# A hybrid decoder layer on one core: the sums from the output projection on move from GpSimd to VectorE, and the last norm's column sums are written earlier

## The chip, the core and the metric

The kernel runs on one core of a Trainium2 chip. The metric is the device time of one execution in microseconds. The engines named below are TensorE (PE in the rows, its weight loads PEld), VectorE (DVE), ScalarE (ACT), GpSimd (POOL) and SyncE (SP, the queue that issues the transfers). Each has its own queue of instructions and works it off in order; semaphores tie the queues together.

## The reference

One layer of a decoder in fp32, 1024 tokens by 1024 channels. The parts that come last, and that the change is about:

```python
h = h + mix @ w_out                                              # output projection
u = rms_norm(h, norm_mlp_g)
h = h + jnp.square(jax.nn.relu(u @ w_up)) @ w_down               # up and down, 4096 wide
gate = jax.nn.sigmoid(rms_norm(h, norm_ple_g) @ w_ple_gate)
h = h + gate * (p @ w_ple)                                       # gate
return rms_norm(h, final_norm_g)                                 # last norm
```

`mix` is the output of eight attention heads and four mLSTM heads; the change does not touch them.

## The kernel before

**Arithmetic.** Activations lie transposed, channels on partitions and tokens along the row, so a tile is 128 channels by 1024 tokens (two halves of 512). Each fp32 operand is kept as a high part and a low part: `split` casts the high part on ScalarE (L92) and takes source minus high part on VectorE (L93). `mm3` (L101 to L103) makes three matmuls of it: high by high, high by low, low by high.

**Seven products.** Up, down and gate are computed in 2x2 blocks with seven products instead of eight. Their keys are b11, t1, t2, b22, t3, b21, t4; the t operands are sums of blocks, on the side of the weights and on the side of the activations. These sums, in SBUF, are what moves:
- `load_blocks` (L754) loads the weights of one output block of up (`wu`, 32 calls) or of the gate (`wpg`) and forms the weight sums, L759 to L761: one of 128x512 and two of 128x256. Those of `wu` run on GpSimd, those of `wpg` on VectorE already. Then it splits a part of 768 columns, which the first products of the next block use, and one of 1024.
- `operands` (L788) forms the sums of h for up, L797: sixteen of 128x512, four after the 4th and four after the 8th output channel block (each on two halves), in the midst of the output projection.
- `weights` (L962) forms, while the down projection runs, the weight sums of 128x1024: L968 for t1 (8), L975 for t2 and b22 (16, each one needs the tile `s` of the key before), L971 for t3 (8). Weights arrive by `wd_r` (four buffers, 512 KB each) and activations by `y_r` (three). A sum frees a buffer of `wd_r`, and SP's next transfer into it waits for that.
- `gate` (L1132) adds the squares for the last norm: L1146, five of them on GpSimd.

**Down.** For each key there are eight steps g; a step takes one tile of weights and one of activations, splits both (`wd`, `y`), and runs 24 matmuls of 128x512. At a key's last step the sums in PSUM are added into h on VectorE (L1085).

**The end.** The last 256 columns of both halves are done last. `final_cols(i)` (L1169) takes column sums on TensorE (`cs`) of one quarter of the tokens, forms their mean on VectorE (`ra`, L1180) and the power on GpSimd (`rb`, L1181). `final(i)` (L1183) spreads `rb` over the partitions by TensorE (`bp`), copies it (`rows`) and multiplies: eight tiles `out`, on VectorE (L1195) for the numbers in `ON_V`, otherwise on ScalarE (L1197) and GpSimd (L1198); then SP writes them out (L1201), 1 MB a quarter.

**Order.** The source is not the order of execution. A scheduler places the instructions of each engine by a simulation of its own at build time; the tile pools add the waits for free buffers. On the chip the order of an engine is fixed.

Of the kernel before, what the change touches and what calls it, by code (L numbers as in the profile page):

```python
# [12 lines left out]
ALU = mybir.AluOpType  # L13
# [3 lines left out]
P = 128  # L17
D = 1024
T = 1024
KT = D // P  # L20
# [25 lines left out]
def layer_kernel(ctx, tc, xT, wqk, wv, wvg, wmv, wmqk, wmo, wout, wup, wdown, wpg, wple, pT,  # L46
                 cols, cosT, sinT, biasT, identT, maskT, lastT, belowT, outT):
    nc = tc.nc
    V, S, G, PE = nc.vector, nc.scalar, nc.gpsimd, nc.tensor
# [3 lines left out]
    op = ctx.enter_context(tc.tile_pool(name="op", bufs=14))  # L53
# [8 lines left out]
    def unit(name, dt=F32R):  # L62
        return op.tile([P, T], dt, name=name, tag="op")
# [24 lines left out]
    def split(hl, src, scale=None):  # L88

        hi, lo = hl  # L90
        if scale is None:
            S.copy(hi, src)  # L92
            V.tensor_tensor(lo, src, hi.bitcast(F32), op=ALU.subtract)  # L93
        else:
            S.activation(hi, src, AF.Copy, scale=scale)
            V.scalar_tensor_tensor(lo, src, scale, hi.bitcast(F32), op0=ALU.mult, op1=ALU.subtract)
        return hl
# [87 lines left out]
    for i in range(2):  # L185
        raw = unit("wr", F32)
        w0.append([wp.tile([P, WT], F32R, name="wqk_" + t, tag="w" + t) for t in "hl"])
        for at in ((slice(0, 256), slice(256, T)) if i == 0 else (slice(0, T),)):
# [7 lines left out]
            if i == 0 and at.start == 0:  # L196
                x0 = pair("x")
                for c in range(NCH):
                    sl = slice(c * CH, (c + 1) * CH)
# [4 lines left out]
    for k in range(KT):  # L204
# [5 lines left out]
        eng = G if k in (1, 3) else V  # L210
# [310 lines left out]
    L = 2 * P  # L521
# [192 lines left out]
    with ExitStack() as tail:  # L714
# [36 lines left out]
        WI = dict(b11=0, t1=1, t2=2, b21=3, t4=4, t3=5, b22=6)  # L751
        BANK = dict(b11="x", t1="z", t2="x", b22="z", t3="x", b21="y", t4="x")

        def load_blocks(src, name, raw=None, pool=None, eng=G):  # L754
            if raw is None:
                raw = wtc.tile([P, 8, L], F32, name=name + "_r", tag="wc", bufs=2)
            if src is not None:
                nc.sync.dma_start(raw[:, :4], src)
            eng.tensor_tensor(raw[:, 4:7:2], raw[:, 2:3].to_broadcast([P, 2, L]), raw[:, 1:4:2], op=ALU.subtract)  # L759
            eng.tensor_tensor(raw[:, 5], raw[:, 3], raw[:, 4], op=ALU.subtract)  # L760
            eng.tensor_tensor(raw[:, 7], raw[:, 0], raw[:, 5], op=ALU.subtract)  # L761
            wa = split(wtile(name, 3, "wa", pool), raw[:, 3:6])
            wb = wtile(name, 4, "wb", pool)
            split([t.rearrange("p (a b) l -> p a (b l)", b=2) for t in wb],
                  raw.rearrange("p (a b) l -> p a (b l)", b=2)[:, 0::3])
            return wa, wb
# [21 lines left out]
        def operands(src, new, temp):  # L788

            ts = {k: temp("t") for k in ("t1", "t3", "t2", "t4")}  # L790
            c0, c1 = slice(0, CH), slice(CH, T)
            for key, i0, s0, i1, s1, o in (("t1", 0, c1, 0, c0, ALU.subtract), ("t2", 1, c1, "t1", None, ALU.add),
                                           ("t3", 0, c1, 1, c1, ALU.add), ("t4", 1, c0, "t2", None, ALU.subtract)):
                for u in range(2):
                    us = slice(u * CH, (u + 1) * CH)
                    in1 = ts[i1][:, us] if s1 is None else src[u][i1][:, s1]
                    G.tensor_tensor(ts[key][:, us], src[u][i0][:, s0], in1, op=o)  # L797
            x = {}
            for key in OPS:
                hl = x[key] = new()  # L800
                if key in ts:
                    split(hl, ts[key])
                    continue
                i, at = dict(b11=(0, c0), b21=(1, c0), b22=(1, c1))[key]
                for u in range(2):
                    us = slice(u * CH, (u + 1) * CH)
                    split((hl[0][:, us], hl[1][:, us]), src[u][i][:, at])
            return x
# [56 lines left out]
        for k2 in range(KT // 2):  # L865
            e = ztile("emb")
            for i in range(2):
                k = 2 * k2 + i
# [91 lines left out]
        sw = [sp4[g // 2][g % 2] for g in range(NG)]  # L960

        def weights(key, g):  # L962

            if key in ("b11", "b21", "t4"):
                return wraw(g, dict(b11=A11, b21=A12, t4=A22)[key])
            if key == "t1":
                a, b = wraw(g, A21), wraw(g, A22)
                G.tensor_tensor(sw[g], a, b, op=ALU.subtract)  # L968
            elif key == "t3":
                a, b = wraw(g, A21), wraw(g, A11)  # L970
                G.tensor_tensor(a, a, b, op=ALU.subtract)  # L971
                return a
            else:
                a = wraw(g, dict(t2=A11, b22=A12)[key])
                G.tensor_tensor(sw[g], a, sw[g], op=ALU.subtract)  # L975
            return sw[g]

        h = [unit("h", F32) for _ in range(KT)]
# [81 lines left out]
        for key in D_OPS:  # L1060
# [4 lines left out]
            i, c = TO_C[key]  # L1065
            for g in range(NG):
# [5 lines left out]
                if (key, g) in LOADS:  # L1072

                    k, half_of = LOADS[key, g]
                    G.tensor_copy(h[k][:1, half_of.start:half_of.start + 1], yl.bitcast(F32)[:1, :1])
                    nc.sync.dma_start(h[k][:, half_of], hs[k, :, half_of])
                for o in range(KT // 2):
                    for u in range(2):
                        at = slice((2 * o + u) * P, (2 * o + u + 1) * P)
                        us = slice(u * CH, (u + 1) * CH)  # L1080
# [14 lines left out]
                if (key, g) == ("t4", 5):  # L1095
                    raws = [act.tile([P, 2, T], F32, name="wpg_r", tag="act").rearrange("p a (b l) -> p (a b) l", l=L)
                            for _ in range(2)]
                    for i in range(2):
# [4 lines left out]
        wt0, wt1, wcp, xb = [tail.enter_context(tc.tile_pool(name=n, bufs=b, reuse_waits="tile"))  # L1103
                             for n, b in (("wt0", 1), ("wt1", 1), ("wcp", 2), ("xb", 4))]
# [3 lines left out]
        fin = state  # L1108
        wblocks = {}

        def fetch(o):
            wblocks[o] = []
            for i in range(2):
                if o == 0:
                    raw, src = raws[i], None
                else:
                    raw, src = wcp.tile([P, 8, L], F32, name="wpg_r", tag="wc"), wpg[o, i]
                    if o == 1:

                        G.tensor_copy(raw[:1, 0, :1], X[i]["t4"][1].bitcast(F32)[:1, :1])  # L1120
                wblocks[o].append(load_blocks(src, "wpg", raw, (wt0, wt1)[i], V))

        def fetch_emb(o):
            ahead = unit("e", F32) if o == 0 else None
# [7 lines left out]
        def gate(k, sl, src, ga):  # L1132
            c = sl.start // CH
            at = slice(sl.start - c * CH, sl.stop - c * CH)
            V.tensor_tensor(ga, src, rB[:, sl], op=ALU.mult)
            S.activation(ga, ga, AF.Tanh, scale=0.5)
            V.scalar_tensor_tensor(ga, ga, 1.0, emb[k, c][:, at], op0=ALU.add, op1=ALU.mult)
            V.scalar_tensor_tensor(h[k][:, sl], ga, 0.5, h[k][:, sl], op0=ALU.mult, op1=ALU.add)
            if k == 0:
                S.activation(fin[:, sl], h[k][:, sl], AF.Square)  # L1140
                return
            S.activation(ga, h[k][:, sl], AF.Square)
            if k == KT - 1:
                last[sl.start] = ga
            else:
                (G if c and k < 6 else V).tensor_tensor(fin[:, sl], fin[:, sl], ga, op=ALU.add)  # L1146

        def embed(o, off=0, n=CH, hooks={}):
            tmp = {}
# [19 lines left out]
        def final_cols(i):  # L1169
            sl = FINAL[i]  # L1170
            nt = (sl.stop - sl.start) // P
            cs = acc_tile("cs3")
            for j in range(nt):
                for src in (fin[:, sl], last[sl.start]):
                    PE.matmul(cs[:, j:j + 1], src[:, j * P:(j + 1) * P], ones, start=src is not last[sl.start],
                              stop=src is last[sl.start])
            a = zp.tile([P, nt], F32, name="ra3", tag="ra")
            b = cols_of[i] = zp.tile([P, nt], F32, name="rb3", tag="rb")
            at = slice(sl.start // P, sl.stop // P)
            V.scalar_tensor_tensor(a, cs[:, :nt], 1.0 / D, seps[:, at], op0=ALU.mult, op1=ALU.add)  # L1180
            G.tensor_tensor(b, a, mhalf[:, :nt], op=ALU.pow)  # L1181

        def final(i):  # L1183
            sl = FINAL[i]
            n = sl.stop - sl.start
            bp = acc_tile("bp3")
            bcast_rows(bp, cols_of[i], n // P)
            rows = small("rows")[:, :n]
            S.copy(rows, bp[:, :n])
            outs = wcp.tile([P, 8, L], F32, name="out", tag="wc")  # L1190
            for k in range(KT):
                o = outs[:, k]
                gain = col[:, C_GFIN + k:C_GFIN + k + 1]
                if k in ON_V[i]:
                    V.scalar_tensor_tensor(o, h[k][:, sl], gain, bp[:, :n], op0=ALU.mult, op1=ALU.mult)  # L1195
                else:
                    S.mul(o, h[k][:, sl], gain)  # L1197
                    G.tensor_tensor(o, o, rows, op=ALU.mult)  # L1198
                if k + 1 in TO[i]:
                    k0 = max(t for t in (0,) + TO[i] if t <= k)  # L1200
                    nc.sync.dma_start(outT[k0:k + 1, :, sl].rearrange("k p t -> p k t"), outs[:, k0:k + 1])  # L1201

        ON_V = ((0, 1, 3, 4, 6), (0, 1, 3, 4, 5, 6), range(KT), (0, 2, 3, 5, 6, 7))
        TO = ((4, 8), (4, 8), (4, 8), (2, 4, 6, 8))
        FINAL = [slice(c * CH + a, c * CH + a + L) for a in (0, L) for c in (1, 0)]

# [8 lines left out]
        for o in range(1, NO - 1):  # L1215
# [4 lines left out]
        fetch_emb(NO - 1)  # L1220
        embed(NO - 1, 0, L)
        embed(NO - 1, L, L, hooks={"b11": [lambda: final_cols(0)], "b22": [lambda: final(0)],
                                   "t3": [lambda: final_cols(1)], "t4": [lambda: final(1), lambda: final_cols(2)]})
        final(2)
        final_cols(3)
        final(3)


def _tables():
# [78 lines left out]
```

## Time and profile before

| | |
|---|---|
| median of 3 runs | 1397.48 us (1396.22 to 1398.34) |
| profiled execution | 1397.32 us, span 1395.5 us |
| output projection, late half | about 583 to 627 us of the span |
| embedding product `pl` | about 627 to 650 us |
| up | about 650 to 985 us |
| down | about 985 to 1290 us |
| gate | about 1295 to 1376 us |
| last norm and output | to 1395.5 us |

In the page's busy times VectorE counts the time in which an instruction is held, as well as that in which it works; GpSimd's spans are rough. The clock of TensorE that the throttle granted stands in the rows of stretches as 1.00 (2.4 GHz) or 0.50 (1.2 GHz).

### The profile page before, as it was taken

Reading aid. Unit: us, or ns where it says so; the run is one execution under the profiler, and the core shown is the slowest. Engines: PE = TensorE matmul, PEld = TensorE weight load, DVE = VectorE, ACT = ScalarE, POOL = GpSimd, SP = SyncE. Lnnn points to the kernel's source line nnn. Section 1 sums busy time; section 2 is a strip of 40 time slices with the busy share of each in tenths; the row PEclk is TensorE's granted clock in tenths of the full one; section 3 lists DMA queues with packets and bytes.
Section 4 is the critical chain, followed back from the end, with each engine's and each line's share of the span. In section 5 each row is a group of like instructions: output and inputs, shape, how many; then the busy total and the mean of one; then the engine's idle time right before and its main releaser. Section 6 shows DMA issues by size and latency. Waiting matters only on the chain.

```text
span 1395.5 us, 18439 instructions
## 1 busy us (share of the span) xinstructions
PE 1337.2 (96%) x6795; PEld 1121.1 (80%) x6795; DVE 1018.9 (73%) x1558; ACT 654.7 (47%) x1036; POOL 408.2 (29%) x271
## 2 busy tenths in 40 slices
PE   8999999999979999999999999999999899999995
PEld 6978988977868887787888888888887688888875
DVE  7788679589859796597566676567558965778896
ACT  6556545644446343256443334435334233465553
POOL 1432031142103222056333443332006771311012
PEclk9999999999999999999999999999999999999997
DMA  6111012222225347554164444446869674481323
GB/s 231 46 50 37 22 51 62 61 91 84 76 71 196 128 138 241 200 185 179 46 223 154 166 157 175 151 152 253 322 231 322 245 247 144 151 301 61 106 83 128
DMA packets 79017, 208.25 MB, mean 149 GB/s; under 512 B 7536, under 2 KB 19728, under 8 KB 74320
## 3 DMA queue, kind: packets, MB, share of 16 engines
q1 hardware_dynamic: 78928, 207.09, 43.1%
q8 instruction: 53, 0.87, 0.3%
q14 instruction: 36, 0.29, 0.1%
HBM read 146.74 MB, written 60.32 MB: 148 GB/s over the span
## 4 chain that ended last, share of the span: by engine, by line
PE 50%; DVE 11%; DMA 7%; issue 3%; POOL 2%; ACT 2%; SPq 0%; DVEq 0%; POOLq 0%; ACTq 0%
PE u L102 7%; PE u L103 7%; PE u L101 7%; PE d L102 6%; PE d L103 6%; PE d L101 6%; DMA wd_r<-wdown 2%; DMA w<-arow 1%; DMA wpg_r<-wpg 1%; POOL s L968 1%; DVE yl L93 1%; DMA in<-mixmd 1%; PE mo L101 1%; PE o L103 1%; PE mo L103 1%
## 5 line engine op out<-in xcount | busy, mean ns | idle before, releaser
L102 PE MATMUL u<-x,wuh 128*128 128x512 f32 x448 | 178.4, 398 | 0.2 <-DVE x L93 0.2
L101 PE MATMUL u<-x,wuh 128*128 128x512 f32 x448 | 176.0, 398 | 1.5 <-ACT x L92 1.5
L102 PE MATMUL d<-yl,wdh 128*128 128x512 f32 x432 | 169.0, 392 | 7.3 <-DVE yl L93 7.3
L103 PE MATMUL u<-x,wul 128*128 128x512 f32 x448 | 173.4, 398 | 0.0
L103 PE MATMUL d<-yh,wdl 128*128 128x512 f32 x432 | 168.3, 391 | 0.0
L101 PE MATMUL d<-yh,wdh 128*128 128x512 f32 x432 | 166.6, 391 | 0.0
L93 DVE TENSOR_TENSOR wul<-wu_r,wuh 128x768 fp32r<-128x768 f32 (+1 forms) x64 | 72.3, 1130 | 78.8 <-ACT wuh L92 78.8
L101 PEld LDWEIGHTS u<-x,wuh 128*128 128x128 f32 x448 | 84.9, 190 | 22.6 <-ACT x L92 2.4
L102 PEld LDWEIGHTS d<-yl,wdh 128*128 128x128 f32 x432 | 81.5, 189 | 25.9 <-DVE yl L93 8.9
L102 PEld LDWEIGHTS u<-x,wuh 128*128 128x128 f32 x448 | 85.0, 190 | 20.7 <-DVE x L93 0.5
L759 POOL TENSOR_TENSOR wu_r<-wu_r 128x512 f32<-128x512 f32 x32 | 47.0, 1468 | 186.3 <-DMA wu_r<-wup 161.2
L103 PEld LDWEIGHTS u<-x,wul 128*128 128x128 f32 x448 | 85.0, 190 | 20.1
L92 ACT CAST wuh<-wu_r 128x768 fp32r<-128x768 f32 (+1 forms) x64 | 60.5, 946 | 78.7 <-POOL wu_r L760 55.2
L103 PEld LDWEIGHTS d<-yh,wdl 128*128 128x128 f32 x432 | 81.6, 189 | 16.9
L101 PEld LDWEIGHTS d<-yh,wdh 128*128 128x128 f32 x432 | 81.4, 189 | 16.9
L93 DVE TENSOR_TENSOR yl<-y_r,yh 128x1024 fp32r<-128x1024 f32 x54 | 89.8, 1664 | 0.0
L93 DVE TENSOR_TENSOR wdl<-wd_r,wdh 128x1024 fp32r<-128x1024 f32 x30 | 42.5, 1416 | 51.3 <-ACT wdh L92 51.3
L412 ACT ACTIVATE pr<-pr,mn 128x128 f32<-128x128 f32 (+3 forms) x64 | 49.5, 774 | 56.0 <-PE av L415 30.4
L92 ACT CAST wdh<-wd_r 128x1024 fp32r<-128x1024 f32 x30 | 31.5, 1051 | 73.4 <-PE d L102 54.2
L92 ACT CAST wdh<-s 128x1024 fp32r<-128x1024 f32 x24 | 25.2, 1048 | 84.1 <-issue 70.5
L911 ACT COPY tmp<-u 128x512 f32<-128x512 f32 x48 | 28.0, 586 | 77.9 <-PE u L103 77.9
L93 DVE TENSOR_TENSOR wdl<-s,wdh 128x1024 fp32r<-128x1024 f32 x24 | 37.3, 1555 | 36.1 <-ACT wdh L92 36.1
(398 smaller groups left out, 3754.0 us busy)
## 6 DMA issues: line engine op xcount, KB each, us to landing
wd_r<-wdown SPq DMA_DIRECT2D x72, 512.0 KB
y_r<-zd SPq DMA_DIRECT2D x56, 512.0 KB
wu_r<-wup SPq DMA_DIRECT2D x32, 512.0 KB
zd<-zz SPq DMA_DIRECT2D x16, 1024.0 KB
zd<-zt SPq DMA_DIRECT2D x16, 1024.0 KB
wm_r<-wmqk SPq DMA_DIRECT2D x8, 512.0 KB
wo_r<-wout SPq DMA_DIRECT2D x16, 256.0 KB
hs<-h SPq DMA_DIRECT2D x8, 512.0 KB
```

The source lines that it names most:

```text
L92: S.copy(hi, src)
L93: V.tensor_tensor(lo, src, hi.bitcast(F32), op=ALU.subtract)
L101: PE.matmul(ps, wh, xh, start=start, stop=False, skip_group_check=more)
L102: PE.matmul(ps, wh, xl, start=False, stop=False, skip_group_check=more)
L103: PE.matmul(ps, wl, xh, start=False, stop=stop, skip_group_check=more)
L412: S.activation(pr[:, :nk], pr[:, :nk], AF.Exp, scale=-1.0, bias=mn[:, :1], accum_out=den)
L759: eng.tensor_tensor(raw[:, 4:7:2], raw[:, 2:3].to_broadcast([P, 2, L]), raw[:, 1:4:2], op=ALU.subtract)
L911: S.copy(tmp[key], ps)
L968: G.tensor_tensor(sw[g], a, b, op=ALU.subtract)
```

## The change

All sums named above go to VectorE: `load_blocks` loses its argument for the engine, `operands`, `weights` and `gate` call `V`. What stays on GpSimd from there on are the powers (L831, L833, L1181), copies of one element that hold back a load (L1075, L1120), and products of the last norm (L1198). For quarter 2 VectorE takes five tiles `out` instead of eight; for quarter 1 still six, of which one is another. `final(1)` moves from the hook of the last product to the end, and `final_cols(3)` before it.

```diff
@@ -751,14 +751,14 @@
-        def load_blocks(src, name, raw=None, pool=None, eng=G):
+        def load_blocks(src, name, raw=None, pool=None):
             if raw is None:
                 nc.sync.dma_start(raw[:, :4], src)
-            eng.tensor_tensor(raw[:, 4:7:2], raw[:, 2:3].to_broadcast([P, 2, L]), raw[:, 1:4:2], op=ALU.subtract)
-            eng.tensor_tensor(raw[:, 5], raw[:, 3], raw[:, 4], op=ALU.subtract)
-            eng.tensor_tensor(raw[:, 7], raw[:, 0], raw[:, 5], op=ALU.subtract)
+            V.tensor_tensor(raw[:, 4:7:2], raw[:, 2:3].to_broadcast([P, 2, L]), raw[:, 1:4:2], op=ALU.subtract)
+            V.tensor_tensor(raw[:, 5], raw[:, 3], raw[:, 4], op=ALU.subtract)
+            V.tensor_tensor(raw[:, 7], raw[:, 0], raw[:, 5], op=ALU.subtract)
             wa = split(wtile(name, 3, "wa", pool), raw[:, 3:6])
@@ -794,7 +794,7 @@
                     in1 = ts[i1][:, us] if s1 is None else src[u][i1][:, s1]
-                    G.tensor_tensor(ts[key][:, us], src[u][i0][:, s0], in1, op=o)
+                    V.tensor_tensor(ts[key][:, us], src[u][i0][:, s0], in1, op=o)
             x = {}
@@ -965,14 +965,14 @@
                 a, b = wraw(g, A21), wraw(g, A22)
-                G.tensor_tensor(sw[g], a, b, op=ALU.subtract)
+                V.tensor_tensor(sw[g], a, b, op=ALU.subtract)
             elif key == "t3":
                 a, b = wraw(g, A21), wraw(g, A11)
-                G.tensor_tensor(a, a, b, op=ALU.subtract)
+                V.tensor_tensor(a, a, b, op=ALU.subtract)
                 return a
                 a = wraw(g, dict(t2=A11, b22=A12)[key])
-                G.tensor_tensor(sw[g], a, sw[g], op=ALU.subtract)
+                V.tensor_tensor(sw[g], a, sw[g], op=ALU.subtract)
             return sw[g]
@@ -1118,7 +1118,7 @@
                         G.tensor_copy(raw[:1, 0, :1], X[i]["t4"][1].bitcast(F32)[:1, :1])
-                wblocks[o].append(load_blocks(src, "wpg", raw, (wt0, wt1)[i], V))
+                wblocks[o].append(load_blocks(src, "wpg", raw, (wt0, wt1)[i]))
@@ -1143,7 +1143,7 @@
             else:
-                (G if c and k < 6 else V).tensor_tensor(fin[:, sl], fin[:, sl], ga, op=ALU.add)
+                V.tensor_tensor(fin[:, sl], fin[:, sl], ga, op=ALU.add)
@@ -1200,7 +1200,7 @@
-        ON_V = ((0, 1, 3, 4, 6), (0, 1, 3, 4, 5, 6), range(KT), (0, 2, 3, 5, 6, 7))
+        ON_V = ((0, 1, 3, 4, 6), (0, 1, 3, 4, 6, 7), (0, 1, 3, 4, 6), (0, 2, 3, 5, 6, 7))
         TO = ((4, 8), (4, 8), (4, 8), (2, 4, 6, 8))
@@ -1220,10 +1220,10 @@
         embed(NO - 1, L, L, hooks={"b11": [lambda: final_cols(0)], "b22": [lambda: final(0)],
-                                   "t3": [lambda: final_cols(1)], "t4": [lambda: final(1), lambda: final_cols(2)]})
-        final(2)
+                                   "t3": [lambda: final_cols(1)], "t4": [lambda: final_cols(2)]})
         final_cols(3)
-        final(3)
+        for i in range(1, 4):
+            final(i)
```

Three places show how the order of VectorE changes. First the down projection, where key b21 ends and t1 begins. L93 are the low parts (`wdl` of weights, `yl` of activations, in the order of their steps), `s_8967` to `s_8970` the sums of two steps each. VectorE before:

```order
L93 TENSOR_TENSOR wdl_9534<-wd_r_9531,wdh_9533 128x1024
L93 TENSOR_TENSOR yl_9528<-y_r_9525,yh_9527 128x1024
L93 TENSOR_TENSOR wdl_9591<-s_8967,wdh_9590 128x1024
L93 TENSOR_TENSOR yl_9582<-y_r_9579,yh_9581 128x1024
L93 TENSOR_TENSOR wdl_9630<-s_8967,wdh_9629 128x1024
L1085 TENSOR_TENSOR h_8971<-h_8971,d_9261 128x512
L93 TENSOR_TENSOR yl_9621<-y_r_9618,yh_9620 128x1024
L1085 TENSOR_TENSOR h_8973<-h_8973,d_9262 128x512
L1085 TENSOR_TENSOR h_8975<-h_8975,d_9263 128x512
L1085 TENSOR_TENSOR h_8977<-h_8977,d_9264 128x512
```

and now:

```order
L968 TENSOR_TENSOR s_8968<-wd_r_9663,wd_r_9665 128x1024
L93 TENSOR_TENSOR wdl_9591<-s_8967,wdh_9590 128x1024
L968 TENSOR_TENSOR s_8968<-wd_r_9704,wd_r_9706 128x1024
L93 TENSOR_TENSOR yl_9582<-y_r_9579,yh_9581 128x1024
L93 TENSOR_TENSOR wdl_9630<-s_8967,wdh_9629 128x1024
L968 TENSOR_TENSOR s_8969<-wd_r_9745,wd_r_9747 128x1024
L1085 TENSOR_TENSOR h_8971<-h_8971,d_9261 128x512
L93 TENSOR_TENSOR yl_9621<-y_r_9618,yh_9620 128x1024
L1085 TENSOR_TENSOR h_8973<-h_8973,d_9262 128x512
L1085 TENSOR_TENSOR h_8975<-h_8975,d_9263 128x512
L968 TENSOR_TENSOR s_8969<-wd_r_9786,wd_r_9788 128x1024
L1085 TENSOR_TENSOR h_8977<-h_8977,d_9264 128x512
```

The sums L968 for the steps of t1 stand between the low parts and between the additions into h (L1085) of the key before, each about one step ahead of the low part `wdl` that reads it.

Next a cycle of up, where `zz` and `zt` are the results of the block before and `wu_r_7731`, `wu_r_7744` the two weight tiles of the next. VectorE before:

```order
L891 SCALAR_TENSOR_TENSOR zz_7464<-zz_7464,rB_7034 128x2048
L896 TENSOR_TENSOR zt_7591<-zz_7464 128x512
L898 TENSOR_TENSOR zt_7591<-zz_7464 128x512
L919 TENSOR_TENSOR zz_7597<-tmp_7666,u_7639 128x512
L93 TENSOR_TENSOR wul_7737<-wu_r_7731,wuh_7736 128x768
L897 TENSOR_TENSOR zt_7591<-zz_7464,zt_7591 128x512
L93 TENSOR_TENSOR wul_7750<-wu_r_7744,wuh_7749 128x768
```

and now:

```order
L891 SCALAR_TENSOR_TENSOR zz_7464<-zz_7464,rB_7034 128x2048
L759 TENSOR_TENSOR wu_r_7731<-wu_r_7731 128x2x256
L759 TENSOR_TENSOR wu_r_7744<-wu_r_7744 128x2x256
L760 TENSOR_TENSOR wu_r_7731<-wu_r_7731 128x256
L760 TENSOR_TENSOR wu_r_7744<-wu_r_7744 128x256
L761 TENSOR_TENSOR wu_r_7731<-wu_r_7731 128x256
L896 TENSOR_TENSOR zt_7591<-zz_7464 128x512
L898 TENSOR_TENSOR zt_7591<-zz_7464 128x512
L761 TENSOR_TENSOR wu_r_7744<-wu_r_7744 128x256
L919 TENSOR_TENSOR zz_7597<-tmp_7666,u_7639 128x512
L93 TENSOR_TENSOR wul_7737<-wu_r_7731,wuh_7736 128x768
```

The six sums of the next block's weights stand between the stores of the block before; the second L759 stands ahead of work that does not read its tile.

Last the end, after the last product's additions; `h_8978` and `ga_12107` belong to the last tile, `bp3` to a quarter. VectorE before:

```order
L1195 SCALAR_TENSOR_TENSOR out_12118<-h_8971,col_70,bp3_12113 128x256
L1195 SCALAR_TENSOR_TENSOR out_12118<-h_8972,col_70,bp3_12113 128x256
L1195 SCALAR_TENSOR_TENSOR out_12118<-h_8974,col_70,bp3_12113 128x256
L1195 SCALAR_TENSOR_TENSOR out_12118<-h_8975,col_70,bp3_12113 128x256
L1195 SCALAR_TENSOR_TENSOR out_12118<-h_8976,col_70,bp3_12113 128x256
L1195 SCALAR_TENSOR_TENSOR out_12118<-h_8977,col_70,bp3_12113 128x256
L1137 SCALAR_TENSOR_TENSOR ga_12087<-ga_12087,e_11828 128x256
L1138 SCALAR_TENSOR_TENSOR h_8978<-ga_12107,h_8978 128x256
L1180 SCALAR_TENSOR_TENSOR ra3_12136<-cs3_12131,seps_80 128x2
L1138 SCALAR_TENSOR_TENSOR h_8977<-ga_12087,h_8977 128x256
L1146 TENSOR_TENSOR state_8979<-state_8979,ga_12087 128x256
```

and now:

```order
L1138 SCALAR_TENSOR_TENSOR h_8977<-ga_12087,h_8977 128x256
L1137 SCALAR_TENSOR_TENSOR ga_12107<-ga_12107,e_11830 128x256
L1138 SCALAR_TENSOR_TENSOR h_8978<-ga_12107,h_8978 128x256
L1146 TENSOR_TENSOR state_8979<-state_8979,ga_12087 128x256
L1180 SCALAR_TENSOR_TENSOR ra3_12118<-cs3_12113,seps_80 128x2
L1195 SCALAR_TENSOR_TENSOR out_12136<-h_8971,col_70,bp3_12131 128x256
L1195 SCALAR_TENSOR_TENSOR out_12136<-h_8972,col_70,bp3_12131 128x256
L1180 SCALAR_TENSOR_TENSOR ra3_12127<-cs3_12122,seps_80 128x2
L1195 SCALAR_TENSOR_TENSOR out_12136<-h_8974,col_70,bp3_12131 128x256
L1195 SCALAR_TENSOR_TENSOR out_12136<-h_8975,col_70,bp3_12131 128x256
L1195 SCALAR_TENSOR_TENSOR out_12136<-h_8977,col_70,bp3_12131 128x256
```

The six `out` of quarter 1 stood ahead of the last L1137 and L1138; now they stand behind them and behind the last L1146, and the mean (L1180) of a later quarter stands among them.

## Rows read from the trace of the kernel before

**Rows 1.** page, busy time: engine, us (share of the span), instructions
```profile
PE 1337.2 (96%) x6795; PEld 1121.1 (80%) x6795; DVE 1018.9 (73%) x1558; ACT 654.7 (47%) x1036; POOL 408.2 (29%) x271
```

**Rows 2.** waits of TensorE, whole span: us in total, times, longest
```profile
PE d L102 <- DVE yl L93: 7.3, 4, 3.5
...
PE bp L130 <- POOL rb L1181: 6.8, 3, 3.2
...
PE u L101 <- ACT x L92: 1.5, 1, 1.5
...
PE pg L101 <- ACT wpgh L92: 1.2, 1, 1.2
```

**Rows 3.** timeline of VectorE, 1076 to 1102 us: start, us, instruction, [idle before]
```profile
1076.98 1.21 DVE L93 TENSOR_TENSOR yl<-y_r,yh 128x1024 fp32r<-128x1024 f32 x1
...
1079.25 5.90 DVE L93 TENSOR_TENSOR yl<-y_r,yh 128x1024 fp32r<-128x1024 f32 x1
...
1093.17 8.22 DVE L93 TENSOR_TENSOR yl<-y_r,yh 128x1024 fp32r<-128x1024 f32 x1
```

**Rows 4.** timeline of GpSimd, 1046 to 1102 us
```profile
1046.60 2.94 POOL L968 TENSOR_TENSOR s<-wd_r 128x1024 f32<-128x1024 f32 x1 [5.18 <-DMA wd_r<-wdown]
...
1079.33 4.74 POOL L975 TENSOR_TENSOR s<-wd_r,s 128x1024 f32<-128x1024 f32 x2
...
1093.25 7.05 POOL L975 TENSOR_TENSOR s<-wd_r,s 128x1024 f32<-128x1024 f32 x3
```

**Rows 5.** stretches: busy us of each engine, granted clock (PEclk), DMA share, GB/s
```profile
580.00:630.00 50.00, 48.41 (x209) 38.59 (x208) 44.02 (x45) 27.49 (x33) 20.05 (x12) 1.00 0.46 158
...
657.65:667.89 10.24, 10.24 (x34) 8.48 (x33) 8.58 (x11) 5.59 (x9) 3.56 (x3) 0.50 0.44 155
...
1101.40:1104.80 3.40, 3.36 (x8) 2.69 (x9) 3.40 (x3) 0.00 (x0) 2.20 (x1) 0.50 0.66 220
...
1391.00:1394.00 3.00, 0.00 (x0) 0.00 (x0) 0.72 (x2) 0.00 (x0) 0.00 (x0) 0.50 1.02 341
```

**Rows 6.** groups of GpSimd by line and shape
```profile
L759 POOL TENSOR_TENSOR wu_r<-wu_r 128x512 f32<-128x512 f32 x32 | 47.0, 1468 | 186.3 <-DMA wu_r<-wup 161.2 <-DVE zz L891 23.7 <-DVE zt L898 1.2
...
L975 POOL TENSOR_TENSOR s<-wd_r,s 128x1024 f32<-128x1024 f32 x16 | 45.6, 2859 | 10.8 <-DVE wdl L93 10.7
...
L761 POOL TENSOR_TENSOR wu_r<-wu_r 128x256 f32<-128x256 f32 x32 | 36.3, 1134 | 1.3
...
L971 POOL TENSOR_TENSOR wd_r<-wd_r 128x1024 f32<-128x1024 f32 x8 | 24.9, 3117 | 65.9 <-DMA wd_r<-wdown 59.3 <-DVE state L998 6.6
...
L968 POOL TENSOR_TENSOR s<-wd_r 128x1024 f32<-128x1024 f32 x8 | 22.3, 2785 | 16.5 <-DMA wd_r<-wdown 15.5 <-PE d L102 0.9
```

**Rows 7.** groups of VectorE by line and shape
```profile
L93 DVE TENSOR_TENSOR yl<-y_r,yh 128x1024 fp32r<-128x1024 f32 x54 | 89.8, 1664 | 0.0
...
L93 DVE TENSOR_TENSOR wul<-wu_r,wuh 128x1024 fp32r<-128x1024 f32 x32 | 39.2, 1224 | 61.9 <-ACT wuh L92 61.9
...
L919 DVE TENSOR_TENSOR zz<-tmp,u 128x512 f32<-128x512 f32 x51 | 33.3, 677 | 7.0 <-ACT tmp L917 3.6 <-PE u L103 3.5
```

**Rows 8.** timeline of TensorE, at 656 us
```profile
656.23 0.49 PE L101 MATMUL u<-x,wuh 128*128 128x512 f32 x1 [1.53 <-ACT x L92]
```

**Rows 9.** timeline of VectorE in the up projection, one f
```profile
792.80 0.94 DVE L93 TENSOR_TENSOR wul<-wu_r,wuh 128x768 fp32r<-128x768 f32 x1
```

**Rows 10.** timeline of TensorE, first use of that low part
```profile
795.29 0.40 PE L103 MATMUL u<-x,wul 128*128 128x512 f32 x1
```

**Rows 11.** timeline of the tail, all engines
```profile
1376.02 16.10 SPq L1201 DMA_DIRECT2D outT<-out  x9
...
1378.62 2.42 DVE L1195 SCALAR_TENSOR_TENSOR out<-h,col,bp 128x256 f32<-128x256 f32 x6
...
1383.98 3.22 DVE L1195 SCALAR_TENSOR_TENSOR out<-h,col,bp 128x256 f32<-128x256 f32 x8 [0.96 <-ACT rows L1189]
...
1389.28 2.44 DVE L1195 SCALAR_TENSOR_TENSOR out<-h,col,bp 128x256 f32<-128x256 f32 x6 [2.01 <-issue]
```

## The prediction

> **What bounds the kernel now.** I began with the page's busy times: TensorE is busy for 1337.2 of 1395.5 us, VectorE for 1018.9, GpSimd for 408.2 [rows 1]. So at most some 58 us of idle TensorE can be won back anywhere, plus what it loses at a lower clock; the sums that leave GpSimd (176 us in the five groups of [rows 6] alone) are worth nothing by themselves. Next I read who makes TensorE wait. From the output projection on four waits stand out: 7.3 us in down for the low part `yl`, 6.8 us in the tail for the power `rb`, 1.5 us at the start of up for `x`, 1.2 us in the gate for a weight's high part [rows 2].
>
> Then I looked at what VectorE does while TensorE waits for `yl`. One `yl` takes 1.21 us, but three others take 5.90, 5.90 and 8.22 [rows 3]. GpSimd's timeline explains the size: 0.08 us after such a `yl` begins, a run of sums L975 begins, two in 4.74 us or three in 7.05 [rows 4], and `yl` ends about 1.2 us after that run. VectorE's subtraction of two SBUF tiles stands still until GpSimd's whole run of back-to-back sums is over. It shows over the whole of down: 54 `yl` take 1664 ns on average against 1210 alone [rows 7, 3].
>
> At two places the granted clock falls to 0.50, the 1.2 GHz level, right after TensorE had stood: for 10.24 us at 657.65 and for 3.40 us at 1101.4 [rows 5]. At 2.4 GHz the same work takes half, so 5.1 and 1.7 us hang on these waits too.
>
> The end is bound otherwise. The last writes run at 341 GB/s with the transfer engines full (share 1.02) [rows 5].
>
> **What VectorE takes on.** GpSimd's sums take 2859, 3117 and 2785 ns for 128x1024, 1468 for 128x512 and 1134 for 128x256 [rows 6]; like operations take VectorE 1224 and 677 ns [rows 7], and 256 columns about 0.40 (six in 2.42) [rows 11]. So:
> - up: 32 x (0.68 + 2 x 0.40) = 47 us,
> - operands: 16 x 0.68 = 11 us,
> - down: 32 x 1.22 = 39 us,
> - gate: 5 x 0.68 = 3 us.
>
> Together 100 us more work, in stretches where VectorE now also stands blocked: the 54 `yl` alone lose 54 x (1.664 - 1.21) = 24 us. VectorE stays below TensorE in up and down. The question is where its order makes TensorE wait.
>
> **Down, t1 and t2: -9 us.** The waits of 7.3 us for `yl` go, since no GpSimd sum is left beside it, and with them 1.7 us for the 3.40 us at half clock. What is late next? A step of 24 matmuls takes 24 x 48.41/209 = 5.6 us [rows 5]; VectorE needs 3 x 1.22 = 3.7 us a step for a sum, `wdl` and `yl`, and between b21 and t1 four additions more (4 x 0.68 = 2.7) and small work. In the new order the sums stand a step ahead of the `wdl` that reads them, and the additions into h stand behind the fifth sum. Each sum waits for two transfers of 512 KB; behind it wait `yl`, `wdl` and those additions, and TensorE behind these. Before, such waits stood on GpSimd: 15.5 us over the sums L968, the largest that I show 5.18 [rows 6, 4]. Laying VectorE's new order by hand against the old landings, at the durations above, I find each sum in time, the fifth barely (an estimate). Bounds: all of 9 is won, or half (4.5) if the additions come late. Below zero is the first rival's.
>
> By the Trainium skill ("SBUF — State Buffer", Who interferes with whom) a VectorE instruction with two SBUF inputs contends with a GpSimd instruction that reads SBUF, and who comes first holds the shared ports for one whole instruction. Rows 3 and 4 agree that it is all or nothing, but not on the length: by one instruction a `yl` would lose at most 2.4 us (4.74/2), and three of them 7.1; measured is 4.7 + 4.7 + 7.0 = 16.4. By the page's measure TensorE's step, with 5.6 us for 3.4 of VectorE's work, would have hidden all but a little of it and this term would be near 2 us; the measurement decides.
>
> **Start of up: -4 us.** TensorE stood 1.5 us at 656.23 for `x`, whose source was a GpSimd sum L797 [rows 2, 8], and then ran 10.24 us at half clock. In the output projection VectorE is busy for 44.02 of 50 us [rows 5]; sixteen sums add 11 us over 585 to 655 us, and what was blocked there comes back. It keeps pace, with eight PSUM banks as slack. But the weights' sums L759 now stand in VectorE's queue among the low parts of `x`, and wait there for `wu` transfers that SP now issues behind others. Laid out by hand in the same way, `x` comes 3 us earlier than before, and the second group of operands some 2 us later than TensorE could use it (estimates). Best: wait and half clock all gone, -7. Worst: as before, 0. I take -4, since one short wait, and a short time at half clock, may remain.
>
> **Up, from the third block: 0.** TensorE is never idle here. The low part of the first weight tile comes at 793.7 and is first read at 795.29 [rows 9, 10], 1.6 us of slack. The six sums (3 us) in VectorE's order come partly into the time in which it waited or stood blocked, and I find this low part 1.1 us later, the second one as before. So the cover is 0.5 us; each 0.5 us beyond it costs 14 blocks x 0.5 = 7 us. Gained can be nothing.
>
> **Gate: -1 us.** Of the 1.2 us wait [rows 2] the part that a GpSimd sum caused goes. Bounds -1.5 and, if the 3 us of new sums come between the evictions, +2.5.
>
> **Tail: -0.5 us.** VectorE drops three tiles for quarter 2 (eight took 3.22 us, six take 2.42 [rows 11]: 1.2 us) and no longer waits for `rb` twice, since the column sums are done earlier; of the 6.8 us [rows 2] some 3.4 stood on VectorE too (0.96 and 2.01 show [rows 11]). That speaks for -4. But `final(1)` goes behind all additions: 3 MB are then left to write, not 2. The last additions end 2.4 us earlier (the six tiles stood before them [rows 11]), near 1380.6; with the first half quarter done the first write is issued near 1383.4. 3 MB at 341 GB/s take 9.2 us, and some 2.3 us lie before the first byte and after the last: 1394.9, against 1395.5. Bounds -2.5 (first issue 2 us earlier) and +2.5 (as much later, or holes between writes).
>
> **Sum.** 1397.32 (the profiled execution, 0.16 under the median, so I use it for the median) - 9 - 4 - 0 - 1 - 0.5 = 1382.8.
>
> **Rivals.**
> 1. *VectorE takes over GpSimd's waits for transfers.* Its queue is in order, so a sum that waits for `wd_r` holds `yl`, `wdl` and the additions. For: GpSimd waited 15.5 us at the eight L968 and 59.3 at the eight L971 [rows 6], 1.9 each at L968. Against: a step leaves VectorE 5.6 - 3.7 = 1.9 us, as much as such a wait, and at L971 GpSimd was simply early. If L968 pass their waits on entire (15.5), L971 half as much each (7.6), and one more stretch runs at half clock as in rows 5 (1.7): 1382.8 + 24.8 = 1407.6. It decides from 14.5 us of passed-on waits on, the whole gain.
> 2. *Only down is won.* The start of up is set by the `wu` transfers, which now hold VectorE, the clock falls as before, and the tail is bound by writing: 1397.3 - 9 + 0.5 = 1388.8 (0.5 for gate and tail together, the middles of their bounds). For: rows 5, last row; VectorE's 44 of 50 us. Against: the operand sums on GpSimd were plainly late.
> 3. *What is won is given back* in up or the gate: VectorE's second L759 waits for its transfer ahead of work that doesn't read it, 1 us beyond the cover for 14 blocks: +14, so 1382.8 + 14 = 1397. For: only 0.5 us of cover. Against: the sum's wait ends when the transfer lands, which before set the same low part.
>
> **Chances.** The forecast 0.60, rival 2 0.16, rival 3 0.10, rival 1 0.14. A measurement of this kernel can tell 0.2%, 2.8 us. Faster: forecast and rival 2, and a little of rival 3: 0.77; within 0.2%: most of rival 3 and a little of rival 1: 0.10; slower: the rest, 0.13. The forecast's own range: the best bounds give 1397.3 - 9 - 7 - 1.5 - 2.5 = 1377.3, the worst 1397.3 - 4.5 - 0 + 2.5 + 2.5 = 1397.8. All of a kind at once is unlikely, but something unseen may be won as well; 1376 to 1397 takes in rivals 2 and 3 and leaves out rival 1.
>
> **What would show it.** Right: in t1 of down each `yl` takes 1.2 us, TensorE has no gap near 1076 to 1102, and the clock stays at 1.00 there; `x` at the start of up comes without a wait of GpSimd's; GpSimd busy under 235 us (408.2 - 176). Wrong: waits of VectorE L968 or L759 for DMA with a TensorE gap a step later (rivals 1, 3); 0.50 still near 657 us (rival 2); the last write more than 12 us after its quarter 1's first one.

## The result, and the profile after

The changed kernel takes 1385.22 us (median of 4 runs, 1384.65 to 1386.07) against 1397.91 us (4 runs, 1396.22 to 1400.28): ratio 0.9908, 95% interval 0.9891 to 0.9926. It is faster by 12.7 us; 14.5 were forecast, and the time lies in the range. The profiled execution took 1386.07 us, its span 1384.3.

From the page of the changed kernel, busy times; they answer to [rows 1]:

```profile
PE 1329.0 (96%) x6795; PEld 1116.8 (81%) x6795; DVE 1023.0 (74%) x1704; ACT 655.4 (47%) x1039; POOL 177.3 (13%) x125
```

VectorE has 146 instructions more and is busy for only 4 us more. What it took on is about 100 us; its other instructions are some 85 us shorter in sum (the records overlap a little), `yl` by 24 us and the stores `zt` of up (L896 to L898) by 23. For `yl` the rows show that it had stood beside GpSimd [rows 3, 4]; for the others I take it to be the same. The groups of VectorE by line and shape, against [rows 6, 7]:

```profile
L93 DVE TENSOR_TENSOR yl<-y_r,yh 128x1024 fp32r<-128x1024 f32 x54 | 65.7, 1217 | 0.0
...
L759 DVE TENSOR_TENSOR wu_r<-wu_r 128x512 f32<-128x512 f32 x32 | 22.1, 692 | 22.7 <-DMA wu_r<-wup 22.2
...
L975 DVE TENSOR_TENSOR s<-wd_r,s 128x1024 f32<-128x1024 f32 x16 | 19.3, 1220 | 5.2 <-DMA wd_r<-wdown 5.2
...
L971 DVE TENSOR_TENSOR wd_r<-wd_r 128x1024 f32<-128x1024 f32 x8 | 9.8, 1224 | 11.7 <-DMA wd_r<-wdown 11.7
L968 DVE TENSOR_TENSOR s<-wd_r 128x1024 f32<-128x1024 f32 x8 | 9.8, 1224 | 10.1 <-DMA wd_r<-wdown 10.0
```

`yl` is at 1217 ns instead of 1664, and the moved sums take what VectorE needs alone for such shapes. The last column has what rival 1 feared: VectorE does wait for transfers, 10.0 + 11.7 + 5.2 us in down, 22.2 in up.

Who makes TensorE wait, from the whole span's list; it answers to [rows 2]:

```profile
PE d L101 <- ACT wdh L92: 3.7, 1, 3.7
...
PE cs L1175 <- DVE state L1146: 3.2, 3, 1.7
...
PE pg L101 <- DVE ga L1159: 2.3, 2, 1.8
PE bp L130 <- POOL rb L1181: 1.8, 1, 1.8
...
PE d L101 <- DVE h L1085: 0.9, 1, 0.9
```

The wait for `yl` is gone, and that for `x`. The first line is a wait that the kernel before did not have. Three stretches (the columns of [rows 5]): the start of up, where the clock had been at 0.50; one at the start of down; and the stretch where the long `yl` had been:

```profile
657.65:667.89 10.24, 10.24 (x51) 8.28 (x51) 8.61 (x14) 6.34 (x10) 2.22 (x2) 1.00 0.30 92
992.80:996.20 3.40, 3.20 (x8) 2.52 (x9) 1.97 (x2) 0.15 (x1) 1.35 (x3) 0.50 0.72 254
1076.00:1102.00 26.00, 26.00 (x117) 21.52 (x116) 20.75 (x19) 10.01 (x10) 9.30 (x3) 1.00 0.74 270
```

TensorE is busy without a hole in the first and the third, at the full clock; in the second it now runs at half clock, right behind the new wait.

Where the 11.3 us between the two spans lie, from the start of the first and last matmul of each stage in the two timelines (before, after, difference):

| stage | before | after | |
|---|---|---|---|
| up to the output projection's late half (not touched) | 581.76 | 583.60 | +1.8 |
| output projection and `pl` | 68.60 | 67.64 | -1.0 |
| up, first to last matmul | 322.56 | 315.80 | -6.8 |
| down, first to last matmul | 315.95 | 312.65 | -3.3 |
| gate | 87.04 | 86.58 | -0.5 |
| last product to the end | 19.20 | 17.56 | -1.6 |

The difference in the first row is spread, of code that the change does not touch: over the kernels below that row lies between 579.2 and 585.3 us. I therefore compare stages, not ends. By these matmuls down begins at 973.1 us in the kernel before and at 967.3 in the changed one, not at about 985 as the table of times ahead of the prediction has it.

### The profile page after: what moved, and what is told of

The parts are those of the page before. It is cut to its first block, busy times and chain, and to the rows that moved or that the text cites. A ratio compares the mean times of both kernels' runs of the same rounds, so it can differ in the third digit from the quotient of the medians.

```text
span 1384.3 us, 18408 instructions
## 1 busy us (share of the span) xinstructions
PE 1329.0 (96%) x6795; PEld 1116.8 (81%) x6795; DVE 1023.0 (74%) x1704; ACT 655.4 (47%) x1039; POOL 177.3 (13%) x125
## 4 chain that ended last, share of the span: by engine, by line
PE 56%; DVE 10%; DMA 6%; issue 2%; ACT 2%; POOL 1%; SPq 0%; DVEq 0%; POOLq 0%; ACTq 0%
PE u L102 8%; PE u L103 8%; PE u L101 8%; PE d L101 7%; PE d L102 7%; PE d L103 7%; PE o L103 1%; PE o L101 1%; PE o L102 1%; DMA wpg_r<-wpg 1%; DMA qw<-arow 1%; DMA wd_r<-wdown 1%; DMA in<-mixmd 1%; PE pg L103 1%; PE pg L101 1%
## 5 line engine op out<-in xcount | busy, mean ns | idle before, releaser
L93 DVE TENSOR_TENSOR wul<-wu_r,wuh 128x768 fp32r<-128x768 f32 (+1 forms) x64 | 69.6, 1087 | 65.6 <-ACT wuh L92 65.4
L1075 POOL COPY h<-yl 1x1 f32<-1x1 f32 x16 | 19.9, 1262 | 444.1 <-DVE yl L93 444.1
L93 DVE TENSOR_TENSOR wdl<-wd_r,wdh 128x1024 fp32r<-128x1024 f32 x30 | 36.6, 1220 | 42.0 <-ACT wdh L92 42.0
L93 DVE TENSOR_TENSOR yl<-y_r,yh 128x1024 fp32r<-128x1024 f32 x54 | 65.7, 1217 | 0.0
L407 DVE CUSTOM_DVE_ANT_0 pr<-s,biasS 128x512 f32<-128x512 f32 (+2 forms) x96 | 51.0, 550 | 12.5 <-PE tp L422 8.9
L92 ACT CAST yh<-y_r 128x1024 fp32r<-128x1024 f32 x54 | 56.5, 1047 | 6.7 <-DMA y_r<-zd 6.7
```

Of the source, the lines that this page charges most:

```text
L407: V.tensor_tensor_reduce(pr[:, ks], s[:, :n], biasS[:, b0 + o:b0 + o + n], 1.0, -2 * LOW, op0=ALU.add, op1=ALU.min, accum_out=mn[:, o // C ...
```

## The experiments

**Down's sums back on GpSimd.** One edit in the changed kernel:

```diff
-                V.tensor_tensor(sw[g], a, b, op=ALU.subtract)
+                G.tensor_tensor(sw[g], a, b, op=ALU.subtract)
...
-                V.tensor_tensor(a, a, b, op=ALU.subtract)
+                G.tensor_tensor(a, a, b, op=ALU.subtract)
...
-                V.tensor_tensor(sw[g], a, sw[g], op=ALU.subtract)
+                G.tensor_tensor(sw[g], a, sw[g], op=ALU.subtract)
```

> The changed kernel, with the 32 weight sums of down (L968, L971, L975) on GpSimd again; all else stays changed. Theory (a GpSimd sum holds VectorE's yl, and TensorE waits for yl): yl's mean goes from 1217 ns back to about 1650, three or four yl of 5 to 9 us stand beside runs of L975, TensorE waits about 7 us for yl, and the time is 1385.2 + 7 to 9 less the 1.3 us gap that the fifth sum makes, 1391 to 1393. Rival (down gained through the earlier start of up and its transfers, not through these sums): 1385 to 1387, with no more than 2 us of waits for yl.

Measured: 1396.15 us (10 runs, ratio to before 0.9973, 0.9959 to 0.9988), above the 1391 to 1393 expected; the profiled execution 1393.07. Down takes 321.8 us, 9.1 more than changed. TensorE's waits in down, both:

```profile
PE d L102 <- DVE yl L93: 7.4, 4, 3.5
PE d L101 <- ACT wdh L92: 3.7, 1, 3.7
```

The first returned as it was in [rows 2]; the second, the new one, stayed. So the sums are worth 9.1 us of down, the new wait has another cause, and the rival falls.

**Down's sums alone on VectorE**, the reverse edit in the kernel before.

```diff
-                G.tensor_tensor(sw[g], a, b, op=ALU.subtract)
+                V.tensor_tensor(sw[g], a, b, op=ALU.subtract)
...
```

> The kernel before, with the 32 weight sums of down alone (L968, L971, L975) on VectorE. Theory (down's gain is its own: no GpSimd sum beside yl): down takes 306 to 308 us instead of 316, since ScalarE's order of casts at its start stays that of before; the start of up keeps its wait and its half clock; about 1397.9 - 9 = 1388 to 1390. Rival (VectorE takes over GpSimd's waits for wd_r, and only the earlier start of up hid that): waits of TensorE of 1 to 3 us in t1 and t3, 1393 or more.

Measured: 1388.47 us (8 runs, ratio 0.9939, 0.9919 to 0.9959). Down takes 305.9 us, 10.0 less than before, and TensorE never stands in it, as the row of that stretch shows (306 us, PE busy throughout, clock 1.00):

```profile
978.16:1284.10 305.94, 305.94 (x1356) 253.22 (x1355) 218.37 (x229) 140.50 (x162) 25.35 (x17) 1.00 0.68 236
```

VectorE takes over GpSimd's waits for `wd_r` (24.0 us in down) and TensorE pays nothing for them here: rival 1 of the prediction is out.

**Both groups of up back on GpSimd**, the sums of `wu` and the operand sums.

```diff
+            eng = G if name == "wu" else V
-            V.tensor_tensor(raw[:, 4:7:2], ...
+            eng.tensor_tensor(raw[:, 4:7:2], ...
...
-                    V.tensor_tensor(ts[key][:, us], src[u][i0][:, s0], in1, op=o)
+                    G.tensor_tensor(ts[key][:, us], src[u][i0][:, s0], in1, op=o)
```

> The changed kernel, with the weight sums of up (L759 to L761 for wu) and the operand sums (L797) on GpSimd again; the weight sums of down stay on VectorE. Theory (the operand sums on GpSimd made x late, and the half clock followed that wait): the wait for x near 655 us and about 10 us at 0.50 come back, +6.5 to +7.5 by the start of down; ScalarE's order of casts at the start of down becomes that of before, so the gap of 4.1 us there and the 3.4 us at half clock behind it go, about -5; 1386 to 1388. Rival A (the gap at the start of down is made by transfers, whatever the order): 1391 to 1393. Rival B (the start of up is won by the order of the transfers): 1380 to 1382.

Measured: 1388.16 us (4 runs, ratio 0.9915, 0.9885 to 0.9945). Up takes 322.0 us (+6.2 on the changed kernel), output projection and `pl` 69.6 (+1.9); down takes 305.9, and its new wait is gone. The half clock at the start of up came back, but for 3.4 us and not 10. The row of that stretch, and TensorE's waits from 630 to 680 us:

```profile
658.20:661.60 3.40, 3.40 (x10) 2.82 (x11) 3.40 (x5) 3.04 (x4) 0.00 (x0) 0.50 0.20 77
...
PE u L101 <- ACT x L92: 2.0, 2, 1.5
PE pl L103 <- DVE wpll L93: 1.6, 1, 1.6
PE u L102 <- DVE x L93: 0.9, 3, 0.5
```

Of the 6.2 us the two waits of `u` make 2.9 and the half clock about 1.7 (half of 3.4, an estimate); the rest I cannot place. So the wait at the start of down hangs on where up's sums run, though nothing of down differs in the source.

**One group of the two.** Only the sums of `wu` back (the first part of that edit):

> The changed kernel, with only the weight sums of up (L759 to L761 for wu) on GpSimd again; the operand sums L797 stay on VectorE. Theory (the late x came from the operand sums, the gap at the start of down from the order of casts that the weight sums on VectorE bring): the start of up as in the changed kernel, up 316 us, no gap of 4 us in down; 1385.2 - 5 to 6 = 1379 to 1381. Rival (the weight sums on GpSimd hold VectorE's low parts of x): the wait near 655 us and the half clock return, up 321 to 323 us, and the time is 1385 to 1388, as with both groups back.

Measured: 1387.75 us (6 runs, ratio 0.9930, 0.9900 to 0.9960); up 322.9 us, down 305.9. My theory of which sums matter fell: the sums of `wu` on GpSimd alone bring the loss at the start of up back. Its GpSimd and VectorE timelines there (its lines stand one further down than before's):

```profile
652.76 2.27 POOL L760 TENSOR_TENSOR wu_r<-wu_r 128x512 f32<-128x512 f32 x1
655.10 1.33 POOL L761 TENSOR_TENSOR wu_r<-wu_r 128x256 f32<-128x256 f32 x1
656.51 1.07 POOL L762 TENSOR_TENSOR wu_r<-wu_r 128x256 f32<-128x256 f32 x1
```

```profile
653.80 2.03 DVE L93 TENSOR_TENSOR wul<-wu_r,wuh 128x768 fp32r<-128x768 f32 x1
656.09 3.25 DVE L93 TENSOR_TENSOR x<-h,x 128x512 fp32r<-128x512 f32 x4 [0.25 <-ACT x L92]
```

`wul` takes 2.03 us and four `x` 3.25 beside them (0.95 and 2.5 without): late low parts again, this time because of the weight sums. Only the operand sums back (the second part):

> The changed kernel, with only the operand sums (L797) on GpSimd again; the weight sums of up stay on VectorE. Theory: x is late again, up takes 321 to 323 us, and the gap at the start of down stays, 1385.2 + 6 = 1390 to 1392. Rival (the weight sums were what held x): the start of up as in the changed kernel, 1385 to 1386.

Measured: 1390.76 us (10 runs, ratio 0.9962, 0.9940 to 0.9983); up 321.4 us, and the wait at the start of down is there (3.7 us). Either group on GpSimd costs the 6 us of up; the two are not added, and both have to move. The gain ahead of up comes with the sums of `wu` alone: output projection and `pl` take 67.6 us here and 70.1 with those sums back. The wait in down, too, comes with the sums of `wu` on VectorE: every kernel that has them there has it until its casts are put in order, and no other.

**The order of casts at the start of down.** ScalarE's order, changed kernel (cut to the first words; the numbers name buffers):

```
L92 CAST wdh_9153<-wd_r_9151 128x1024
L92 CAST yh_9147<-y_r_9145 128x1024
L92 CAST wdh_9191<-wd_r_9189 128x1024
L92 CAST yh_9185<-y_r_9183 128x1024
L92 CAST yh_9109<-y_r_9107 128x1024
L92 CAST wdh_9115<-wd_r_9113 128x1024
```

Before, the last two stood ahead of `wdh_9191`. They are the fifth step's operands, `wdh_9191` and `yh_9185` the seventh's, whose buffers TensorE frees when it ends the fourth step. ScalarE's timeline before, where the third row is `wdh_9115` and the fourth `wdh_9191`:

```profile
989.45 1.05 ACT L92 CAST wdh<-wd_r 128x1024 fp32r<-128x1024 f32 x1 [9.60 <-PE d L102]
990.40 2.00 ACT L92 CAST yh<-y_r 128x1024 fp32r<-128x1024 f32 x2
993.35 1.06 ACT L92 CAST wdh<-wd_r 128x1024 fp32r<-128x1024 f32 x1 [0.96 <-DMA zd<-zt]
994.89 1.05 ACT L92 CAST wdh<-wd_r 128x1024 fp32r<-128x1024 f32 x1 [0.48 <-PE d L102]
```

and in the changed kernel:

```profile
984.58 1.05 ACT L92 CAST yh<-y_r 128x1024 fp32r<-128x1024 f32 x1
989.07 1.04 ACT L92 CAST wdh<-wd_r 128x1024 fp32r<-128x1024 f32 x1 [3.43 <-PE d L102]
990.02 1.99 ACT L92 CAST yh<-y_r 128x1024 fp32r<-128x1024 f32 x2
991.91 1.04 ACT L92 CAST wdh<-wd_r 128x1024 fp32r<-128x1024 f32 x1
```

and TensorE's:

```profile
988.87 0.39 PE L103 MATMUL d<-yh,wdl 128*128 128x512 f32 x1
993.00 1.22 PE L101 MATMUL d<-yh,wdh 128*128 128x512 f32 x2 [3.75 <-ACT wdh L92]
```

ScalarE waits until TensorE has ended the fourth step, then casts the seventh's operands, and last those that TensorE stands for. The edit ties the seventh step's casts to the fifth's by copies of one element into the tile that the cast then fills:

```diff
...
+            for b in behind:
+                S.copy(hl[0][:1, :1], b.bitcast(F32)[:1, :1])
             return split(hl, src)
...
+                    late4 = (wh4,) if (key, g) == ("b11", 6) else ()
-                    yh, yl = parts("y", "y", y_load(g, stream("y_r", "yr", 3), key))
-                    wh, wl = parts("wd", "w", weights(key, g))
+                    yh, yl = parts("y", "y", y_load(g, stream("y_r", "yr", 3), key), late4)
+                    wh, wl = parts("wd", "w", weights(key, g), late4)
+                    if (key, g) == ("b11", 4):
+                        wh4 = wh
```

> The changed kernel, with copies of one element on ScalarE that put the casts of the seventh step of down's first key (they wait for a buffer that TensorE frees at the end of the fourth step) behind those of the fifth, as their order was before. Theory (that order alone makes the gap of 4.1 us at 989 us and the 3.4 us at half clock behind it): the gap shrinks to under 1 us, the clock stays at 1.00, 1385.2 - 3.3 - 1.7 = 1380 to 1381. Rival (the fifth step's buffer comes free only when the last store of up has landed, 987.8 us, and the casts come then whatever their order): the gap stays above 3 us, 1384 to 1386.

Measured: 1379.63 us (4 runs, ratio 0.9857, 0.9824 to 0.9890); down 306.4 us instead of 312.7. ScalarE and TensorE there:

```profile
986.71 1.05 ACT L92 CAST wdh<-wd_r 128x1024 fp32r<-128x1024 f32 x1 [1.80 <-DMA zd<-zt]
987.78 0.19 ACT L955 CAST yh<-wdh 1x1 fp32r<-1x1 f32 x1
987.88 0.18 ACT L955 CAST wdh<-wdh 1x1 fp32r<-1x1 f32 x1
988.01 1.05 ACT L92 CAST yh<-y_r 128x1024 fp32r<-128x1024 f32 x1
```

```profile
987.19 0.39 PE L103 MATMUL d<-yh,wdl 128*128 128x512 f32 x1
987.81 0.50 PE L101 MATMUL d<-yh,wdh 128*128 128x512 f32 x1 [0.23 <-ACT wdh L92]
```

The fifth step now waits for the last store of up (`zd<-zt`), and TensorE for 0.23 us. Putting the order back takes the loss away. To see that this is not spread, both kernels once more, side by side:

> The changed kernel as it is, beside the next one on the same chip: 1385.2, within 1.5 us.

> The kernel with the casts back in order, once more: theory, 5 to 6 us under the changed kernel of the same chip, about 1379.6, and 18 us under the kernel before; rival (the gain seen was the spread of the part ahead of the output projection, some 2 us either way), under 3 us.

Measured: 1388.04 us (6 runs, ratio 0.9911, 0.9889 to 0.9933) and 1380.75 us (5 runs, 0.9875, 0.9855 to 0.9896). The first lies 2.8 us above the 1385.2 that I expected within 1.5, and its spread is wide (1379.69 to 1390.24). Its down takes 313.2 us, the other's 306.6. The medians are 7.3 us apart. This version beats both kernels.

**The tail.** The end of the last norm in the changed kernel, put back as it was:

```diff
-                                   "t3": [lambda: final_cols(1)], "t4": [lambda: final_cols(2)]})
-        final_cols(3)
-        for i in range(1, 4):
-            final(i)
+                                   "t3": [lambda: final_cols(1)], "t4": [lambda: final(1), lambda: final_cols(2)]})
+        final(2)
+        final_cols(3)
+        final(3)
```

with `ON_V` of before.

> The changed kernel, with the last norm as before: final(1) in the hook of the last product, final_cols(3) after final(2), ON_V of before. Theory (the tail is bound by writing 3 MB behind the additions against VectorE's tiles in front of them; both come out alike): 1385.2 + 0.5 to 2, 1386 to 1387. Rival (the earlier column sums are what wins: TensorE's waits for rb, 6.8 us before and 1.8 now): +4 to +5, 1389 to 1390.

Measured: 1386.54 us (5 runs, ratio 0.9916, 0.9881 to 0.9951), from the last product to the end 19.5 us instead of 17.6 (18.3 in the changed kernel's repeat). In time the two cannot be told apart; the stage says 1.1 to 1.9 us. Then, on the kernel with the casts in order, only `final(1)` back in the hook, the column sums still early:

> The kernel with the casts back in order, and final(1) in the hook of the last product again; the column sums stay early and ON_V as changed. Theory (the tail is bound by writing 3 MB at 341 GB/s from the first write of quarter 1 on): that write is issued about 2.5 us earlier, but quarter 2's tiles come 2.4 us later and leave a hole, so from the last product to the end 17.8 us become about 17, and the time is 1378 to 1380, not to be told from the 1379.6 of the kernel that it is built on. Rival (VectorE's tiles in front of the additions are what costs): 18.5 us or more, 1380.5 to 1382.

Measured: 1381.6 us (5 runs, ratio 0.9879, 0.9861 to 0.9897); from the last product to the end 19.4 us against 17.8 (18.3 in the repeat). My theory fell. TensorE's longest wait there, and a stretch of 4 us in which nothing is written (the DMA share, next to last, is 0.00):

```profile
PE cs L1181 <- DVE state L1152: 6.2, 3, 4.4
...
1366.00:1370.00 4.00, 2.10 (x9) 1.30 (x8) 2.30 (x7) 1.55 (x4) 2.75 (x4) 0.50 0.00 0
```

Quarter 1's tiles on VectorE hold back the last additions and with them the column sums of quarters 2 and 3, by more than the earlier writes give.

**How long GpSimd holds VectorE.** In the kernel before, each L975 cut in two:

```diff
-                G.tensor_tensor(sw[g], a, sw[g], op=ALU.subtract)
+                for q in range(2):
+                    qs = slice(q * CH, (q + 1) * CH)
+                    G.tensor_tensor(sw[g][:, qs], a[:, qs], sw[g][:, qs], op=ALU.subtract)
```

> The kernel before, with each of the 16 sums L975 on GpSimd cut into two instructions of 512 columns. Theory (a VectorE subtraction of two SBUF tiles stands until GpSimd's whole back-to-back run ends): the three long yl stay at 5.9 to 8.5 us, TensorE's waits for yl at 7 us or more, 1397 to 1400. Rival (the Trainium skill, SBUF — State Buffer, Who interferes with whom: the shared ports are held for one instruction): no yl there above 1.2 + 1.3 = 2.5 us, the waits for yl under 2 us, 1388 to 1391.

Measured: 1405.12 us, above the 1397 to 1400 expected. It is one run, and the stages ahead of the output projection's late half were 3.3 us longer than in the kernel before, so I read nothing from the time. TensorE's waits for `yl` are 8.3 us. GpSimd's and VectorE's timelines (L977 is the cut L975):

```profile
1084.11 5.02 POOL L977 TENSOR_TENSOR s<-wd_r,s 128x512 f32<-128x512 f32 x4
```

```profile
1084.03 6.18 DVE L93 TENSOR_TENSOR yl<-y_r,yh 128x1024 fp32r<-128x1024 f32 x1
```

Four instructions of 1.25 us, and `yl` still ends only 1.1 us after the last. It is the run, not the instruction, that holds.

## Why the prediction was right

- **Down (-9).** Mechanism and size right: 9.1 us by the sums put back, 10.0 by the sums moved alone. Yet the stage gained only 3.3, since a term of +6.3 (312.7 - 306.4) was missing. It is the wait at 989 us (3.75 us, 0.23 with the casts in order), the half clock behind it (3.4 us, which cost about 1.7, an estimate) and 0.91 us of the next point. The step that failed is "Laying VectorE's new order by hand": I laid out VectorE's order and not ScalarE's, though the change moves rows there too, in a stretch that holds none of the moved sums. The "3.4 of VectorE's work" a step, in the paragraph on the ports, has no row (two low parts of 1.21 us [rows 3] are 2.4); the sum does not use it.
- **The fifth sum, "barely".** It was late: it waited for its transfer, the addition L1085 stood behind it, and TensorE stood 0.91 us for that addition until 1061.02 us. VectorE's timeline:

```profile
1059.05 1.23 DVE L968 TENSOR_TENSOR s<-wd_r 128x1024 f32<-128x1024 f32 x1 [1.34 <-DMA wd_r<-wdown]
1060.19 0.68 DVE L1085 TENSOR_TENSOR h<-h,d 128x512 f32<-128x512 f32 x1
```

  This is the mechanism of rival 1, and all that came of it. The changed kernel's repeat has 0.5 us of it, the other kernels none.
- **Start of up (-4).** Too small: -6.8 in up and -1.0 ahead of it. No wait and no half clock were left, which is the "best" of the bounds. The "some 2 us" by which the second operands were to come late did not show. And the cause was half told: the sums of `wu` held VectorE there as much as the operand sums.
- **Up from the third block (0).** Right. VectorE waited 22.2 us for `wu` transfers, and TensorE had no gap in all of up: rival 3 did not come. Rival 2 was wrong on the start of up.
- **Gate (-1).** Not shown. The difference of -0.5 is within the spread: the gate as changed takes 86.4 to 90.0 us over the kernels above, the gate of before 87.0 to 87.3. TensorE stands in it 3.9 us in both kernels: the wait for `wpgh` [rows 2] is gone, but that for `ga` grew from 1.0 to 2.3.
- **Tail (-0.5).** Larger: -1.6 here. Over all kernels the stage takes 17.5 to 18.3 us with `final(1)` at the end and 19.2 to 19.7 with it in the hook, so the gain is clear of the spread. "Bound by writing" was read from the last 3 us of the kernel before. Over a longer stretch its writes had holes; the changed kernel's, in this execution, have none. The rows, before (share 0.67) and changed (1.02):

```profile
1377.00:1393.00 16.00, 4.28 (x22) 3.57 (x22) 11.27 (x32) 3.88 (x10) 4.83 (x7) 0.63 0.67 222
...
1373.60:1382.60 9.00, 0.48 (x2) 0.08 (x1) 4.52 (x12) 1.28 (x3) 3.21 (x5) 0.50 1.02 341
```

  In the changed kernel the last quarter's tiles wait for a buffer that a write must free (VectorE's timeline):

```profile
1377.27 2.44 DVE L1195 SCALAR_TENSOR_TENSOR out<-h,col,bp 128x256 f32<-128x256 f32 x6 [1.58 <-DMA outT<-out]
```

So the total came near partly by luck, by two misses that lie against each other: 3.8 us more won ahead of up and at its start, 6.3 lost at the entry to down.

## What to carry to other kernels

Sums with two SBUF operands on GpSimd were not free work beside a VectorE that does the same: a whole back-to-back run of them was time in which VectorE's instruction stood. Look for such runs, and whether a matmul waits for what stood. When a scheduler makes the order, compare it on every engine that feeds TensorE, over the whole stretch behind the edit, for instructions that moved ahead of an earlier step's and wait for a late buffer; most of the 6.3 us lost here, against 12.7 won in all, came from one such pair. Put such an order right by a dependency, not by hoping that the next edit turns it back.

## What the runs showed of the hardware that was not expected

A run of GpSimd sums holds a VectorE subtraction of two SBUF tiles until its end, also when it is four instructions (6.18 us for 1.21). The Trainium skill ("SBUF — State Buffer", Who interferes with whom) has the lock last one instruction; these runs show longer. And the part ahead of the output projection, the same in all kernels, took between 579.2 and 585.3 us.
